# Moving the node projection behind the last transposition of a sort, in program order

## The chip, the core and the metric

The kernel runs on one core of one Trainium2 chip. The metric is the device time of one execution in microseconds (us), as the median of several runs. A ratio in this document is the mean time of one kernel's fast runs over the mean of the other's fast runs of the same rounds, so it is not quite the ratio of the quoted medians.

The engines are called by their names in the profile: PE is TensorE (PEld its weight loads), DVE is VectorE, ACT is ScalarE, SP is SyncE, whose queue (SPq) issues DMAs here.

## The reference

A message-passing layer over a graph with 4096 nodes and 262,144 edges:

```python
N, E, D = 4096, 262144, 256
self_out = nodes @ w_self
msg = nodes[edges_src] @ w_msg
agg = np.zeros((N, D), dtype=np.float32)
np.add.at(agg, edges_dst, msg)
return self_out + agg
```

## The kernel before

The kernel has three stages. First it loads the edges, packs each edge into one number (key) and brings the 2048 columns of keys into an order with a sorting network. VectorE does the compare steps (minimum and maximum). Now and then the data has to be moved between partitions; TensorE does that by a matmul with a rotated identity matrix, and ScalarE copies the result back. Second, the *projection*: `Y = nodes @ w_msg`, in 32 blocks of 128 rows. It needs the transposed nodes `XT`, which 64 transposing DMAs bring. Third, the counting stage builds one-hot matrices from the sorted keys on VectorE, counts pairs with matmuls, and multiplies the counts with `Y`. The counting stage needs both the end of the sort and `Y`.

The parts that matter here (cuts marked):

```python
# the transposed nodes: 64 DMAs on SyncE's queue                       (line 195)
for t in range(T):                                    # T = 32
    for k in range(2):
        nc.sync.dma_start(
            XT[:, k, t * P:(t + 1) * P],
            nodes_bf_dram[t * P:(t + 1) * P, k * P:(k + 1) * P],
            transpose=True,
        )

psum_y = tc.alloc_tile_pool(name="psum_y", bufs=1, space=bass.MemoryType.PSUM)
for t in range(T):                                    # the projection
    y_ps = psum_y.tile([P, D], FP32, name="y_ps", tag="y_ps", bufs=2)
    for k in range(2):
        nc.tensor.matmul(                             # line 205
            out=y_ps[:], lhsT=XT[:, k, t * P:(t + 1) * P], rhs=wcat[:, 2 + k, :],
            start=(k == 0), stop=(k == 1),
        )
    nc.scalar.copy(out=Y[:, t, :], in_=y_ps[:])       # line 209

psum_sort = tc.alloc_tile_pool(name="psum_sort", bufs=1, space=bass.MemoryType.PSUM)
own = _run_sort(nc, psum_sort, XA, XS, id2, plan, halo)
# ... keys -> run numbers, transpositions, then the counting stage
```

```python
def _run_sort(nc, psum, XA, XS, id2, plan, halo):
    # ...
    for op in SORT_A:
        x, y = XA[a], XA[1 - a]
        if op[0] == "b":
            gap(x, y, op[1])                          # compare steps on VectorE
        # ... "q4": the same idea as below with another view (lines 610, 614)
        elif op[0] == "q16":
            # ...
            for t in range(4):
                tp = psum.tile([P, 512], FP32, name="tp_sw", tag="tp", bufs=4)
                for g in range(4):
                    # ...
                    nc.tensor.matmul(...)             # line 622: a "sort matmul"
                nc.scalar.copy(...)                   # line 626
        # ...
    for t in range(0, nk, 4):                         # the sort's last transposition
        # ...
            nc.tensor.transpose(...)                  # line 645
        nc.scalar.copy(...)                           # line 648
    a = 0
    for h, b, (s0, n0), (s1, n1) in plan:             # VectorE alone, the sort's tail
        # ...
```

The kernel is written against a framework that traces these calls, finds the dependencies and then *emits* one stream of instructions for each engine. The source text is only its input.

Of the kernel before, what the change touches and what calls it, by code (L numbers as in the profile page):

```python
# [9 lines left out]
P = 128  # L10
FP32 = mybir.dt.float32
# [40 lines left out]
def kernel(  # L52
# [9 lines left out]
    nc = tc.nc  # L62

    N, D = nodes.shape
# [4 lines left out]
    T = N // P  # L69
# [13 lines left out]
    wcat = feat.tile([P, 4, D], BF16, name="wcat")  # L83
    XT = feat.tile([P, 2, N], BF16, name="XT")
    Y = feat.tile([P, T, D], BF16, name="Y")
# [7 lines left out]
    plan, halo = _tail_plan(SORT_S)  # L93
    TOT = NCOL + 2 * halo
    sortp = tc.alloc_tile_pool(name="sortp", bufs=1)
    XA = [sortp.tile([P, FP + NCOL + BP], FP32, name=f"XA{i}") for i in range(2)]
    XS = [sortp.tile([P, TOT], FP32, name=f"XS{i}") for i in range(2)]
    id2 = sortp.tile([P, 2 * P], FP32, name="id2")
# [100 lines left out]
            )  # L199

    psum_y = tc.alloc_tile_pool(name="psum_y", bufs=1, space=bass.MemoryType.PSUM)
    for t in range(T):
        y_ps = psum_y.tile([P, D], FP32, name="y_ps", tag="y_ps", bufs=2)
        for k in range(2):
            nc.tensor.matmul(  # L205
                out=y_ps[:], lhsT=XT[:, k, t * P:(t + 1) * P], rhs=wcat[:, 2 + k, :],
                start=(k == 0), stop=(k == 1),
            )
        nc.scalar.copy(out=Y[:, t, :], in_=y_ps[:])  # L209

    psum_sort = tc.alloc_tile_pool(name="psum_sort", bufs=1, space=bass.MemoryType.PSUM)
    own = _run_sort(nc, psum_sort, XA, XS, id2, plan, halo)

    k16 = meta.tile([P, G16], FP32, name="k16")
    k16i = meta.tile([P, G16], I32, name="k16i")
# [19 lines left out]
    own = own[:, halo:halo + NCOL]  # L235
# [20 lines left out]
        out=wr[:], in0=sl[:], scalar1=float(RING), scalar2=float(-RING * BW),  # L256
# [5 lines left out]
        out=poff[:], in0=poff[:], scalar1=2, scalar2=PSUM0,  # L262
        op0=ALU.logical_shift_left, op1=ALU.bitwise_or,
    )
    for t in range(G16 // 4):
        tp = psum_sort.tile([P, 512], FP32, name="tp_sw", tag="tp", bufs=4)
        for k in range(4 * t, 4 * t + 4):
            s = slice(k * P, (k + 1) * P)
            nc.vector.tensor_scalar(
                out=rel[:, s], in0=own[:, s], scalar1=g7f[:, k:k + 1], scalar2=32640.0,  # L270
# [4 lines left out]
            out=vals[:].rearrange("p (q k) -> p q k", k=G16)[:, :, 4 * t:4 * t + 4],  # L275
            in_=tp[:].rearrange("p (k q) -> p q k", k=4),
# [125 lines left out]
    with tc.manual_schedule():  # L402
# [52 lines left out]
        out=bad[0:1, 0:1], in0=gi[0:1, 0:1], scalar=float(W - 1), in1=bad[0:1, 0:1],  # L455
# [7 lines left out]
        out=btot[:], in0=bsum[:, 1:2], scalar=float(E), in1=bsum[:, 0:1],  # L463
# [68 lines left out]
def _tail_plan(gaps):  # L532

    a, e = 0, 2048
    plan = []
    for h in reversed(gaps):
        b = h & -h
        passes = []
        for par in (1, 0):
            i0 = (a - h) // b  # L540
            i0 += (i0 - par) % 2
            i1 = -(-e // b) - 1
            i1 -= (i1 - par) % 2
            passes.append((i0 * b, (i1 - i0) // 2 + 1))
            a = min(a, i0 * b)
            e = max(e, i1 * b + b + h)
        plan.append((h, b, passes[1], passes[0]))
    halo = -(-max(-a, e - 2048) // 128) * 128
    return plan[::-1], halo


def _blocks(x, start, n, b):
    v = x[:, start:start + 1]
    return bass.AP(tensor=v.tensor, offset=v.offset, ap=[list(v.ap[0]), [2 * b, n], [1, b]])


def _run_sort(nc, psum, XA, XS, id2, plan, halo):
    n_col = 2048
    mm = nc.vector.tensor_tensor

    def pair(lo, up, lo_out, up_out):
        mm(out=lo_out, in0=lo, in1=up, op=ALU.min)  # L562
        mm(out=up_out, in0=lo, in1=up, op=ALU.max)  # L563

    def gap(x, y, m):
        b = m & -m
        if m <= PADM:
            n = n_col // (2 * b)
            for par, u in ((0, x), (1, y)):
                s = FP + par * b  # L570
                up = _blocks(u, s + m, n, b)
                pair(_blocks(x, s, n, b), up, _blocks(y, s, n, b), up)
            return
        n = (n_col - m) // b
        k = (n_col - 2 * m) // b
        for par in (0, 1):
            cnt, cin = (n + 1 - par) // 2, (k + 1 - par) // 2
            s, f = FP + par * b, FP + (par + 2 * cin) * b
            lows = [(s, cin), (f, cnt - cin)]
            if par == 0:  # L580
                mm(
                    out=_blocks(y, s, cnt, b), in0=_blocks(x, s, cnt, b),
                    in1=_blocks(x, s + m, cnt, b), op=ALU.min,
                )
            for i, (st, c) in enumerate(lows):
                if not c:
                    continue
                lo = _blocks(x, st, c, b)
                up = _blocks(y if par == 1 and i == 0 else x, st + m, c, b)
                if par == 1:  # L590
                    mm(out=_blocks(y, st, c, b), in0=lo, in1=up, op=ALU.min)
                mm(
                    out=_blocks(x if par == 0 and i == 0 else y, st + m, c, b),
                    in0=lo, in1=up, op=ALU.max,
# [6 lines that stand above are left out]
            gap(x, y, op[1])  # L601
        elif op[0] == "q4":
            bb, rots = op[1:]
# [3 lines that stand above are left out]
                    r = rots[4 * t + g]  # L607
                    c = FP + 512 * t
                    sel = lambda v: v.rearrange("p (i g b) -> p i g b", g=4, b=bb)[:, :, g, :]
                    nc.tensor.matmul(  # L610
                        out=sel(tp[:]), lhsT=id2[:, (P - r) % P:(P - r) % P + P],
                        rhs=sel(x[:, c:c + 512]), start=True, stop=True,
                    )
                nc.scalar.copy(out=y[:, c:c + 512], in_=tp[:])  # L614
        elif op[0] == "q16":
            bb, rots = op[1:]
            sel = lambda v: v[:, FP:FP + n_col].rearrange("p (i g b) -> p g i b", g=16, b=bb)
# [3 lines that stand above are left out]
                    r = rots[4 * t + g]  # L621
                    nc.tensor.matmul(  # L622
                        out=tp[:, g * P:(g + 1) * P], lhsT=id2[:, (P - r) % P:(P - r) % P + P],
                        rhs=sel(x)[:, 4 * t + g], start=True, stop=True,
                    )
                nc.scalar.copy(  # L626
                    out=sel(y)[:, 4 * t:4 * t + 4],
                    in_=tp[:].rearrange("p (g i b) -> p g i b", g=4, b=bb),
                )
        elif op[0] == "sh":  # L630
            bb, mask = op[1:]
            v = x[:, FP:FP + n_col].rearrange("p (i g b) -> p i g b", g=2, b=bb)[:, :, 1, :]
            nc.vector.stream_shuffle(out=v, in_=v, mask=mask)
            continue
        else:
            nc.vector.transpose(out=y[:, FP:FP + n_col], in_=x[:, FP:FP + n_col])
        a = 1 - a
    x = XA[a]
    nk = (n_col + 2 * halo) // P
    for t in range(0, nk, 4):  # L640
        w = min(4, nk - t)
        tp = psum.tile([P, 512], FP32, name="tp_sw", tag="tp", bufs=4)
        for k in range(t, t + w):
            c = FP + k - halo // P
            nc.tensor.transpose(
                tp[:, (k - t) * P:(k - t + 1) * P], x[:, c:c + 16 * (P - 1) + 1:16], id2[:, 0:P]
            )
        nc.scalar.copy(out=XS[0][:, t * P:(t + w) * P], in_=tp[:, 0:w * P])
    a = 0
    for h, b, (s0, n0), (s1, n1) in plan:  # L650
        x, y = XS[a], XS[1 - a]
        for s, n, u in ((halo + s0, n0, x), (halo + s1, n1, y)):
            up = _blocks(u, s + h, n, b)
            pair(_blocks(x, s, n, b), up, _blocks(y, s, n, b), up)
        a = 1 - a
    return XS[a]
# [30 lines left out]
```

## Time and profile before

| | before |
|---|---|
| time, median of 3 (range) | 609.61 us (609.27 to 610.24) |
| span of the profiled run | 606.5 us |
| first compare steps on VectorE end | 69.15 us |
| first sort matmul starts | 117.78 us |
| VectorE goes on with the sort | 124.15 us |
| sort's tail on VectorE | 233.4 to 283 us |
| first one-hot of the counting stage | 292.03 us |

From the page of the kernel before: the span cut into 40 equal slices, each digit the busy share of the slice in tenths.

```profile
span 606.5 us, 10333 instructions
...
PE   0013332410434123001799999999999999999997
...
DVE  3999500079564865999999999898989889898940
```

The right half is the counting stage, with both engines nearly full. On the left VectorE has a hole of three empty slices, from about 76 to 121 us, while TensorE is 20 to 40% busy. The list of waits says what ended it. Each line gives the waiting engine and line, what it waited for, us in total, how often, and the longest single wait.

```profile
PE y_ps L205 <- DMA XT<-nodes_bf_dram: 92.8, 64, 37.2
...
DVE XA L562 <- ACT XA L626: 62.0, 2, 55.0
```

VectorE waited 55.0 us once for ScalarE's copy of a sort matmul. But the copy only came late because the matmul came late. TensorE's timeline around it (start, duration, engine, line, operation; in brackets the idle time before it and what ended that):

```profile
117.59 0.40 PE L205 MATMUL y_ps<-wcat,XT 128*128 128x256 bf16 x1 [0.86 <-DMA XT<-nodes_bf_dram]
117.78 1.53 PE L622 MATMUL tp_sw<-XA,id 128*128 128x128 f32 x6
```

VectorE's timeline:

```profile
68.95 0.20 DVE L592 TENSOR_TENSOR XA<-XA 128x44 f32<-128x44 f32 x1
124.15 1.23 DVE L562 TENSOR_TENSOR XA<-XA 128x1024 f32<-128x1024 f32 x1 [55.00 <-ACT XA L626]
```

The data of the first sort matmul was there at 69.15 us. It started 0.19 us behind the start of the last of the 64 projection matmuls, and it has no idle time of its own: it stood behind them in TensorE's stream. The projection matmuls are not slow, they wait. The views of the lines concerned (durations in ns: least, median, greatest; then the first and the last start in us):

```profile
L205 PE MATMUL y_ps<-wcat,XT x64: 392/393/397, 37.2 to 117.6; 128*128 128x256 bf16 x64
```

```profile
L195 SPq DMA_TRANSPOSE XT<-nodes_bf_dram x64: 1207/1232/1242, 34.8 to 115.2; - x64
```

Each of the 64 transpositions holds its queue for 1.23 us, they start 1.28 us apart ((115.2 − 34.8) / 63), and their data lands 2.3 us after the issue (median). So the last projection matmul can't run before 117.6 us, and whatever stands behind it in TensorE's stream can't either. The Trainium skill ("TensorE: Matmul & The Clock Gate", Part 2) says that matmuls stay in program order, which we read as the order of the engine's own instruction stream. The trace agrees: the first sort matmul, ready at 69.15 us, starts at 117.78 us.

One more thing is to be read from VectorE's timeline: the order in which instructions run is not that of the source. These are two stretches of it.

```profile
26.35 0.77 DVE L581 TENSOR_TENSOR XA<-XA 128x595 f32<-128x595 f32 x1
27.04 0.16 DVE L181 TENSOR_SCALAR ta<-ta 128x16 int32<-128x16 int32 x1
...
27.63 0.17 DVE L185 CUSTOM_DVE_ANT_0 lo_c<-ta,tb 128x32 uint16<-128x32 uint16 x1
...
291.44 0.17 DVE L458 TENSOR_REDUCE bcol<-bad 128x1 f32<-128x16 f32 x1
...
292.03 0.69 DVE L305 TENSOR_TENSOR e_oh<-slo_b,jrow 128x1024 bf16<-128x1024 int16 x1
```

Line 581 belongs to the sort, which the source calls after lines 181 and 185, yet it runs before them. Line 458 stands in the source behind the whole counting stage, yet it runs ahead of that stage's first one-hot (line 305). The framework fills each engine's stream with what is ready.

### The profile page before, as it was taken

Reading aid. Unit: us, or ns where it says so; the run is one execution under the profiler, and the core shown is the slowest. Engines: PE = TensorE matmul, PEld = TensorE weight load, DVE = VectorE, ACT = ScalarE, POOL = GpSimd, SP = SyncE. Lnnn points to the kernel's source line nnn. Section 1 sums busy time; section 2 is a strip of 40 time slices with the busy share of each in tenths; the row PEclk is TensorE's granted clock in tenths of the full one; section 3 lists DMA queues with packets and bytes.
Section 4 is the critical chain, followed back from the end, with each engine's and each line's share of the span. In section 5 each row is a group of like instructions: output and inputs, shape, how many; then the busy total and the mean of one; then the engine's idle time right before and its main releaser. Section 6 shows DMA issues by size and latency. Waiting matters only on the chain.

```text
span 606.5 us, 10333 instructions
## 1 busy us (share of the span) xinstructions
PE 365.0 (60%) x4113; PEld 324.4 (53%) x4113; DVE 461.1 (76%) x388; ACT 274.4 (45%) x792; POOL 9.7 (2%) x28
## 2 busy tenths in 40 slices
PE   0013332410434123001799999999999999999997
PEld 0000000310334123000698989898988989898986
DVE  3999500079564865999999999898989889898940
ACT  2001111110111012000387878777878777787886
POOL 6000000000000000000000000000000000000000
PEclk9999999975657577555699999999999999999999
DMA  9921111000000000000000000000000000000000
GB/s 312 197 80 26 25 25 26 21 0 0 0 0 0 1 1 1 0 0 1 0 2 29 1 28 2 28 2 28 2 28 3 26 28 2 28 1 29 1 28 22
DMA packets 24356, 15.66 MB, mean 26 GB/s; under 512 B 10994, under 2 KB 23794, under 8 KB 23794
## 3 DMA queue, kind: packets, MB, share of 16 engines
q1 hardware_dynamic: 19362, 10.51, 5.8%
q0 software_dynamic: 4656, 2.36, 2.9%
q10 hardware_dynamic: 288, 2.10, 0.9%
q8 instruction: 34, 0.56, 0.4%
q14 instruction: 16, 0.13, 0.1%
HBM read 8.92 MB, written 6.30 MB: 25 GB/s over the span
## 4 chain that ended last, share of the span: by engine, by line
PE 51%; DVE 22%; SPq 13%; DMA 5%; ACT 5%; issue 2%; POOL 1%; ACTq 0%; DVEq 0%; POOLq 0%
PE ring L333 21%; PE out_ps L390 17%; SPq L195 13%; DVE XA L562 6%; DVE XA L563 6%; PE out_ps L385 6%; DVE XS L563 4%; DVE XS L562 4%; ACT at L359 3%; PE tp_sw L610 3%; DMA nodes_bf<-in_nodes_dram 3%; PE tp_sw L622 2%; DMA nodes_bf_dram<-nodes_bf 2%; PE out_ps L378 1%; ACT o_sb L399 1%
## 5 line engine op out<-in xcount | busy, mean ns | idle before, releaser
L359 ACT ACTIVATE at<-ring 128x496 bf16<-128x496 f32 (+1 forms) x352 | 202.0, 574 | 69.7 <-PE ring L333 68.2
L390 PE MATMUL out_ps<-Y,at 128*128 128x256 bf16 x1024 | 169.0, 273 | 0.0
L305 DVE TENSOR_TENSOR e_oh<-slo_b,jrow 128x4096 bf16<-128x4096 int16 (+2 forms) x68 | 147.1, 2164 | 28.8 <-PE ring L333 27.4
L333 PE MATMUL ring<-d_oh,e_oh 128*128 128x112 bf16 x2048 | 164.0, 214 | 2.7 <-DVE d_oh L305 2.7
L333 PEld LDWEIGHTS <-e_oh 128*128 128x128 bf16 x2048 | 138.4, 98 | 6.6 <-issue 2.5
L305 DVE TENSOR_TENSOR d_oh<-rel_b,jrow 128x3584 bf16<-128x3584 int16 (+2 forms) x68 | 129.7, 1907 | 0.0
L390 PEld LDWEIGHTS <-at 128*128 128x128 bf16 x1024 | 99.3, 97 | 8.3
L385 PE MATMUL out_ps<-Y,at 128*128 128x256 bf16 (+1 forms) x351 | 95.2, 271 | 0.0
L333 PE MATMUL ring<-zer 128*128 128x224 bf16 x352 | 91.8, 261 | 0.7 <-ACT vals L274 0.7
L562 DVE TENSOR_TENSOR XA<-XA 128x1024 f32<-128x1024 f32 x15 | 18.4, 1226 | 82.4 <-ACT XA L626 62.0
L205 PE MATMUL y_ps<-wcat,XT 128*128 128x256 bf16 x64 | 25.2, 394 | 92.8 <-DMA XT<-nodes_bf_dram 92.8
L359 ACT ACTIVATION_READ_ACCUMULATOR at<-ring 128x1 f32 x352 | 68.7, 195 | 0.0
L205 PEld LDWEIGHTS <-XT 128*128 128x128 bf16 x64 | 6.7, 104 | 111.0 <-DMA XT<-nodes_bf_dram 111.0
L209 ACT CAST Y<-y_ps 128x256 bf16<-128x256 f32 x32 | 11.9, 372 | 91.3 <-PE y_ps L205 91.3
L610 PE MATMUL tp_sw<-XA,id 128*128 128x128 f32 x96 | 17.6, 365 | 37.7 <-DVE XA L563 37.7
L610 PEld LDWEIGHTS tp_sw<-XA,id 128*128 128x128 f32 x96 | 17.1, 278 | 38.2 <-issue 38.2
L333 PEld LDWEIGHTS <-zer 128*128 128x128 bf16 x352 | 34.7, 98 | 5.0 <-issue 0.9
L273 PE MATMUL tp_sw<-ident,XS 128*128 128x128 f32 x16 | 4.7, 452 | 53.8 <-DVE qb L164 53.8
L385 PEld LDWEIGHTS <-at 128*128 128x128 bf16 (+1 forms) x351 | 34.8, 99 | 1.0 <-issue 0.8
L273 PEld LDWEIGHTS tp_sw<-ident,XS 128*128 128x128 f32 x16 | 2.9, 183 | 55.4 <-issue 54.4
L622 PE MATMUL tp_sw<-XA,id 128*128 128x128 f32 x64 | 11.9, 367 | 31.0 <-DVE XA L563 31.0
L614 ACT COPY XA<-tp_sw 128x512 f32<-128x512 f32 x12 | 7.0, 585 | 48.3 <-PE tp_sw L610 48.3
(99 smaller groups left out, 257.0 us busy)
## 6 DMA issues: line engine op xcount, KB each, us to landing
out_dram<-o_sb SPq DMA_DIRECT2D x11, 256.0 KB, 2.2
s<-in_edges_src_dram ACTq DMA_DIRECT2D x2, 1024.0 KB, 10.2
d<-in_edges_dst_dram SPq DMA_DIRECT2D x2, 1024.0 KB, 10.4
nodes_bf<-in_nodes_dram POOLq DMA_DIRECT2D x1, 2048.0 KB, 17.6
nodes_bf_dram<-nodes_bf SPq DMA_DIRECT2D x1, 2048.0 KB, 9.5
out_dram<-o_sb SPq DMA_DIRECT2D x10, 128.0 KB, 2.1
XT<-nodes_bf_dram SPq DMA_TRANSPOSE x64, 2.3
wcat<-in_w_self_dram POOLq DMA_DIRECT2D x1, 128.0 KB, 12.1
```

Of the source, the lines that this page charges most:

```text
L195: nc.sync.dma_start(XT[:, k, t * P:(t + 1) * P], nodes_bf_dram[t * P:(t + 1) * P, k * P:(k + 1) * P], transpose=True,)
L205: nc.tensor.matmul(out=y_ps[:], lhsT=XT[:, k, t * P:(t + 1) * P], rhs=wcat[:, 2 + k, :], start=(k == 0), stop=(k == 1),)
L209: nc.scalar.copy(out=Y[:, t, :], in_=y_ps[:])
L305: tt(out=o[:, 0:n // 2], in0=val[:, c:c + n].rearrange("p (g i) -> p g i", i=2).unsqueeze(2).to_broadcast(shp), in1=jrow[:, 0:wid, :].unsq ...
L333: mm = nc.tensor.matmul(out=ap, lhsT=lhsT, rhs=rhs, start=start, stop=True, skip_group_check=True,).ins
L359: ins = nc.scalar.activation(out=at[:, 0:n], in_=ring[:, b:b + n], func=ACTF.Copy, accum_out=csum[:, r:r + 1],).ins
L385: nc.tensor.matmul(out=out_ps[0:m, 0, :], lhsT=at_of.pop(r - 1)[:, w:w + m], rhs=Y[:, b, :], start=False, stop=False, skip_group_check=True,)
L390: nc.tensor.matmul(out=out_ps[:, t, :], lhsT=at[:, t * P:(t + 1) * P], rhs=Y[:, b, :], start=False, stop=(b == NB - 1), skip_group_check=True,
L562: mm(out=lo_out, in0=lo, in1=up, op=ALU.min)
L563: mm(out=up_out, in0=lo, in1=up, op=ALU.max)
L610: nc.tensor.matmul(out=sel(tp[:]), lhsT=id2[:, (P - r) % P:(P - r) % P + P], rhs=sel(x[:, c:c + 512]), start=True, stop=True,)
L622: nc.tensor.matmul(out=tp[:, g * P:(g + 1) * P], lhsT=id2[:, (P - r) % P:(P - r) % P + P], rhs=sel(x)[:, 4 * t + g], start=True, stop=True,)
```

## The change

The intent was to close the hole: let the sort matmuls stand ahead of the projection in TensorE's stream. The projection would run under the sort's tail, where TensorE and ScalarE have nothing to do for 50 us. The code of the projection is put into a function, and the sort calls it behind its last transposition.

```diff
-    for t in range(T):
-        y_ps = psum_y.tile([P, D], FP32, name="y_ps", tag="y_ps", bufs=2)
-        ...
-        nc.scalar.copy(out=Y[:, t, :], in_=y_ps[:])
+
+    def project():
+        for t in range(T):
+            y_ps = psum_y.tile([P, D], FP32, name="y_ps", tag="y_ps", bufs=2)
+            ...
+            nc.scalar.copy(out=Y[:, t, :], in_=y_ps[:])
 
     psum_sort = tc.alloc_tile_pool(name="psum_sort", bufs=1, space=bass.MemoryType.PSUM)
-    own = _run_sort(nc, psum_sort, XA, XS, id2, plan, halo)
+    own = _run_sort(nc, psum_sort, XA, XS, id2, plan, halo, project)
@@ _run_sort, behind the loop of the last transposition
         nc.scalar.copy(out=XS[0][:, t * P:(t + w) * P], in_=tp[:, 0:w * P])
+    project()
     a = 0
     for h, b, (s0, n0), (s1, n1) in plan:
```

No operation is added or removed, and no dependency.

More of the change, by code (lines that the diff above doesn't have):

```diff
@@ L201 @@
     psum_y = tc.alloc_tile_pool(name="psum_y", bufs=1, space=bass.MemoryType.PSUM)
-    for t in range(T):
-        y_ps = psum_y.tile([P, D], FP32, name="y_ps", tag="y_ps", bufs=2)
-        for k in range(2):
-            nc.tensor.matmul(
-                out=y_ps[:], lhsT=XT[:, k, t * P:(t + 1) * P], rhs=wcat[:, 2 + k, :],
-                start=(k == 0), stop=(k == 1),
-            )
-        nc.scalar.copy(out=Y[:, t, :], in_=y_ps[:])
+    def project():
+        for t in range(T):
+            y_ps = psum_y.tile([P, D], FP32, name="y_ps", tag="y_ps", bufs=2)
+            for k in range(2):
+                nc.tensor.matmul(
+                    out=y_ps[:], lhsT=XT[:, k, t * P:(t + 1) * P], rhs=wcat[:, 2 + k, :],
+                    start=(k == 0), stop=(k == 1),
+                )
+            nc.scalar.copy(out=Y[:, t, :], in_=y_ps[:])
     psum_sort = tc.alloc_tile_pool(name="psum_sort", bufs=1, space=bass.MemoryType.PSUM)
-    own = _run_sort(nc, psum_sort, XA, XS, id2, plan, halo)
+    own = _run_sort(nc, psum_sort, XA, XS, id2, plan, halo, project)
     k16 = meta.tile([P, G16], FP32, name="k16")
@@ L554, in _blocks, with _run_sort @@
     return bass.AP(tensor=v.tensor, offset=v.offset, ap=[list(v.ap[0]), [2 * b, n], [1, b]])
-def _run_sort(nc, psum, XA, XS, id2, plan, halo):
+def _run_sort(nc, psum, XA, XS, id2, plan, halo, project):
     n_col = 2048
```

## The prediction

> **What bounds the kernel now.** The span is 606.5 us. From about 300 us TensorE is above 90% busy (the 40-slice view); that counting stage is not touched. Before it stands the sort. The list of waits shows its one big hole: VectorE (L562) waits 55.0 us for the ScalarE copy L626. The timeline shows why: VectorE's first run of compare stages ends at 69.15 us, but the first sort matmul (L622) starts at 117.78 us, 0.19 us behind the start of the last projection matmul (L205, 117.59 us). All 64 projection matmuls stand ahead of it in TensorE's stream, and each waits for its DMA transposition (92.8 us in 64 waits; one transposition each 1.27 us, 34.8 to 117.5 us). The Trainium skill ("TensorE: Matmul & The Clock Gate", Part 2) says matmuls stay in program order; the trace agrees. The chain of waits accordingly runs over the transposition queue (13%).
>
> **What the change would be worth if the emitted order followed the program.** The first sort matmuls would start at about 69.3 us instead of 117.8: 48.5 us saved, all on the chain. The projection would lie under VectorE's last sort stage (233.4 to 283 us, 50 us, TensorE and ScalarE idle): 64 matmuls at 0.2 to 0.4 us and 32 copies of 0.37 us, an estimate of 15 to 25 us, hidden. Total about 561 us, an 8% gain.
>
> **Why I do not expect it.** The builder does not emit instructions in program order: it fills each engine's stream with what is ready in its own model of time, and the program order only decides between ready instructions. The trace of before shows it on VectorE: the sort's L581 starts at 26.35 us ahead of L181 and L185 (27.04 and 27.63 us), which the program states earlier; and L449 to L458, which the program states behind the whole counting stage, run at 290.4 to 291.4 us, ahead of its first one-hot (L305, 292.03 us). So a late place in the program does not keep an instruction late. Early on TensorE's only ready work is the projection, and all of it was emitted ahead of L622. With an order by readiness the builder must have believed the transpositions done before the sort's first matmul is ready; that belief does not change with the move. The projection depends on nothing of the sort, so moving its text adds no dependency. I expect the same stream on TensorE and ScalarE: L205 (new line number) ahead of the first sort matmul, the same 55 us wait, nothing removed, added or moved.
>
> **Predicted time: 609.6 us, 8 in 10 between 607 and 612.** Chances: faster by over 2% 0.10, within 2% 0.89, slower by over 2% 0.01.
>
> **What would show it right.** VectorE's wait for the first sort copy stays at about 55 us; the projection matmuls still start from 37.2 to 117.6 us; the first sort matmul still starts at about 117.8 us; the counting stage starts at about 292 us.
>
> **What would show it wrong.** The first sort matmul at about 69 us, the 55 us wait shrunk to about 6.5 us, as the later ones of its kind (6.2 to 7.4 us), the projection matmuls between about 184 and 235 us, and a time near 561 us. That happens if the builder keeps TensorE's order by program for these instructions, or if a PSUM slot or its model's timing holds the projection back until sort matmuls are ready. A partial hoist would give something between.

## The result, and the profile after

| | before | after |
|---|---|---|
| time, median (range), 4 runs each | 609.44 us (609.16 to 610.24) | 607.79 us (606.9 to 609.52) |
| span of the profiled run | 606.5 us | 606.1 us |
| projection matmuls start | 37.2 to 117.6 us | 37.1 to 117.5 us |
| first sort matmul starts | 117.78 us | 117.65 us |
| VectorE's wait before the sort goes on | 55.00 us | 54.79 us |
| first one-hot | 292.03 us | 291.58 us |

The ratio is 0.9974, with a 95% interval of 0.995 to 0.9998: the same within 2%, but with an interval that leaves out 1. The experiments come back to that.

The lines of the kernel after that answer to those of before; its line numbers are 2 higher in these parts. The page:

```profile
span 606.1 us, 10333 instructions
...
PE   0013332410434123001799999999999999999997
...
DVE  3999500089564866999999999898989889898940
```

The waits, with the hole unchanged at 54.8 us:

```profile
PE y_ps L207 <- DMA XT<-nodes_bf_dram: 92.6, 64, 37.1
...
DVE XA L564 <- ACT XA L628: 61.7, 2, 54.8
```

TensorE's and VectorE's timelines at the same place:

```profile
117.46 0.40 PE L207 MATMUL y_ps<-wcat,XT 128*128 128x256 bf16 x1 [0.85 <-DMA XT<-nodes_bf_dram]
117.65 1.75 PE L624 MATMUL tp_sw<-XA,id 128*128 128x128 f32 x7
```

```profile
68.87 0.20 DVE L594 TENSOR_TENSOR XA<-XA 128x44 f32<-128x44 f32 x1
123.86 1.23 DVE L564 TENSOR_TENSOR XA<-XA 128x1024 f32<-128x1024 f32 x1 [54.79 <-ACT XA L628]
```

The projection still stands ahead of the sort matmuls. The two emitted programs were then compared instruction by instruction, on every engine: opcode, operands, PSUM banks (PSUM is the memory that the matmuls write to), waits and signals are equal in all of them. Only source line numbers and generated names differ. The change altered the source and not the program.

### The profile page after: what moved, and what is told of

Read it like the earlier page. It is cut to its first block, busy times and chain, and to the rows that moved or that the text cites. A ratio compares the mean times of both kernels' runs of the same rounds, so it can differ in the third digit from the quotient of the medians.

```text
span 606.1 us, 10333 instructions
## 1 busy us (share of the span) xinstructions
PE 364.7 (60%) x4113; PEld 324.1 (53%) x4113; DVE 461.3 (76%) x388; ACT 274.4 (45%) x792; POOL 9.7 (2%) x28
## 4 chain that ended last, share of the span: by engine, by line
PE 51%; DVE 22%; SPq 13%; DMA 5%; ACT 5%; issue 2%; POOL 1%; ACTq 0%; DVEq 0%; POOLq 0%
PE ring L335 21%; PE out_ps L392 17%; SPq L195 13%; DVE XA L565 6%; DVE XA L564 6%; PE out_ps L387 6%; DVE XS L565 4%; DVE XS L564 4%; ACT at L361 3%; PE tp_sw L612 3%; DMA nodes_bf<-in_nodes_dram 3%; PE tp_sw L624 2%; DMA nodes_bf_dram<-nodes_bf 2%; PE out_ps L380 1%; ACT o_sb L401 1%
## 5 line engine op out<-in xcount | busy, mean ns | idle before, releaser
L275 PEld LDWEIGHTS tp_sw<-ident,XS 128*128 128x128 f32 x16 | 2.9, 182 | 55.5 <-issue 54.4
```

## The experiments

What the framework emits on TensorE up to the counting stage, read from each built kernel, in matmuls and transpositions in order ("sort 1" and "sort 2" are the two groups of 16 of line 622, "sort 3 to 5" the 48 of line 610, "last" the 32 of line 645, "keys" the 16 behind the tail; the profile shows two records for each of these sort matmuls, so a group of 16 appears there as x32):

```
before, after, prio, keep_before:  64 projection, sort 1, sort 2, sort 3 to 5, last, keys
pin, keep_after:                   sort 1, sort 2, sort 3 to 5, last, 64 projection, keys
ahead24:                           48 projection, sort 1, sort 2, sort 3 to 5, last, 16 projection, keys
held:                              sort 1 with 28 projection strewn in behind its 4th, 36 projection,
                                   sort 2, sort 3 to 5, last, keys
```

Two questions were open. First, is the hole on VectorE really nothing but TensorE's issue order, and what is it worth? Second, why did the move of the text not change that order? Theory A: the framework emits what is ready in its own model of time, and program order decides only between ready instructions. The rivals were that something else makes the hole, or that program order or priority decides the order after all. All eight runs gave correct results. The first four kernels ran on one chip, beside 11 runs of the kernel before (608.42 us median, 607.17 to 609.83); the other four on another chip, beside 7 runs of it (607.99 us, 607.24 to 609.59).

### pin: the order edge that the move lacked

```diff
-            nc.tensor.transpose(
+            last = nc.tensor.transpose(
                 tp[:, (k - t) * P:(k - t + 1) * P], x[:, c:c + 16 * (P - 1) + 1:16], id2[:, 0:P]
             )
 ...
-    project()
+    with tc.issue_after(last.ins):     # order of issue on TensorE, no wait
+        project()
```

(`tc` is passed into `_run_sort` for it.)

> The changed kernel plus an order edge (issue order only, no wait): every projection matmul is queued behind the last transposition of the sort on TensorE. Theory A (the 55 us hole is only TensorE's issue order): first sort matmul at about 69.3 us, VectorE's wait before it about 6.5 us, projection between 184 and about 205 us under VectorE's tail, counting stage from about 243 us, time about 561 us (ratio 0.92). Rival B (the hole has another cause, such as a transfer that the sort matmuls or their copies wait for, or the projection can't be hidden in the tail): time between 585 and 610 us.

Measured: 560.13 us median (559.61 to 561.2, 5 runs), ratio 0.9211 (0.9194 to 0.9229). VectorE's timeline at the place of the hole:

```profile
68.94 0.20 DVE L594 TENSOR_TENSOR XA<-XA 128x44 f32<-128x44 f32 x1
75.57 1.23 DVE L564 TENSOR_TENSOR XA<-XA 128x1024 f32<-128x1024 f32 x1 [6.43 <-ACT XA L628]
```

And the view of the line of the projection matmuls in the same kernel:

```profile
L207 PE MATMUL y_ps<-wcat,XT x64: 269/270/273, 183.7 to 197.1; 128*128 128x256 bf16 x64
```

The wait fell from 55.00 to 6.43 us. That is 48.57 us, and the median fell by 48.29 us (608.42 − 560.13). The gain arrives whole, because everything up to the counting stage is one chain: the first one-hot moved from 292.03 to 243.25 us.

```profile
243.25 0.69 DVE L307 TENSOR_TENSOR e_oh<-slo_b,jrow 128x1024 bf16<-128x1024 int16 x1
```

The projection now takes 14.0 us (from its first matmul at 183.71 us to the end of its last copy at 197.75 us, early in a tail that begins at 184.65 us and lasts 50 us) and holds nobody up. Its matmuls take 270 ns instead of 393 each; why was not tested. They now run closely one behind the other on data that is long there, but the sort matmuls, too, take 415 ns early in an unbroken run and 273 ns late in it (last section), so a change of clock is a likely cause. This is the version that beats both kernels. Rival B is out: nothing but the order made the hole.

### after_again and before_again: how far identical programs stray

No edit: the kernel after once more, and the kernel before timed against itself.

> The changed kernel once more. Its emitted instructions equal those of before in opcode, operands, PSUM banks, waits and signals on every engine, source line numbers and instruction names apart. Theory A (same program): ratio 1.000 within 0.3%, and the 0.26% of the first comparison is scatter. Rival B (something in it is really faster): ratio 0.997 again, with an interval that excludes 1.

> The kernel before against itself: shows how far a ratio of identical programs strays from 1. Expected 1.000 within 0.3%.

Measured: after_again 608.17 us (607.52 to 610.01, 6 runs), ratio 1.0001 (0.9982 to 1.0021); before_again 608.17 us (607.75 to 610.06, 6 runs), ratio 1.0007 (0.9987 to 1.0027). The 0.26% of the first comparison did not come back, and no difference between the programs exists that could have made it. It was scatter, though its interval left out 1. The interval came from four runs a side; with differences this small it should not be trusted alone.

### ahead24: part of the projection ahead, part behind

As pin, with the first 24 of 32 row blocks stated ahead of the sort, where the framework keeps them ahead:

```diff
-    def project():
-        for t in range(T):
+    def project(t0=24, t1=T):
+        for t in range(t0, t1):
 ...
+    project(0, 24)
     psum_sort = tc.alloc_tile_pool(name="psum_sort", ...)
```

> As the pinned kernel, but the projection of the first 24 of 32 row blocks stands ahead of the sort's matmuls and only the last 8 are pinned behind them. Theory A (the last transposition that stands ahead decides): the 48th projection matmul started at 97.2 us in before, so the first sort matmul starts at about 97.5 us, VectorE's first wait is about 35 us, and the time is 609.5 minus 20.3, about 589 us. Rival B (any projection ahead costs the whole hole, or none does): 609 or 561 us.

Measured: 587.69 us (586.7 to 589.84, 5 runs), ratio 0.9669 (0.9647 to 0.9692). TensorE's timeline and, below it, VectorE's waits:

```profile
97.52 0.40 PE L207 MATMUL y_ps<-wcat,XT 128*128 128x256 bf16 x1 [0.84 <-DMA XT<-nodes_bf_dram]
97.71 5.04 PE L625 MATMUL tp_sw<-XA,id 128*128 128x128 f32 x32
```

```profile
DVE XA L565 <- ACT XA L629: 40.5, 2, 33.9
```

The first sort matmul starts 0.19 us behind the start of the last projection matmul that stands ahead of it, here the 48th, as in the kernel before behind the 64th. VectorE's wait is 33.9 us, 21.1 less than before. The sort starts when the data of the last projection matmul ahead has come. The time fell by 20.7 us; expected were 20.3.

### keep_after and keep_before: program order kept on purpose

The framework can be told to keep program order for chosen engines. In keep_after this is put around the sort (and with it the moved projection); in keep_before around both the projection at its old place and the sort:

```diff
+    with tc.manual_schedule(engines={mybir.EngineType.PE, mybir.EngineType.Activation}):
-    own = _run_sort(nc, psum_sort, XA, XS, id2, plan, halo, project)
+        own = _run_sort(nc, psum_sort, XA, XS, id2, plan, halo, project)
```

```diff
+    with tc.manual_schedule(engines={mybir.EngineType.PE, mybir.EngineType.Activation}):
-    for t in range(T):
-        y_ps = ...
+        for t in range(T):
+            y_ps = ...
 ...
-    own = _run_sort(nc, psum_sort, XA, XS, id2, plan, halo)
+        own = _run_sort(nc, psum_sort, XA, XS, id2, plan, halo)
```

> The changed kernel with TensorE and ScalarE told to keep program order over the sort and the projection. Theory A (the move failed only because the builder reorders): the projection is emitted behind the sort's last transposition, and the time is as with the pinned kernel, about 561 us. Rival B: the change itself is worthless and this stays at 609 us.

> The kernel before (projection stated ahead of the sort) with TensorE and ScalarE told to keep program order over the projection. Theory A: keeping order is not itself a gain, the place of the text counts once order is kept: 609 us, all 64 projection matmuls from 37 to 118 us, first sort matmul at 117.8 us. Rival B (keeping order helps by itself, by different waits): well under 609 us.

Measured: keep_after 560.97 us (559.35 to 561.84, 4 runs), ratio 0.9216 (0.919 to 0.9242); keep_before 609.48 us (607.32 to 610.28, 4 runs), ratio 1.0009 (0.9982 to 1.0037). The view of the projection's tile in keep_after:

```profile
L207 PE MATMUL y_ps<-wcat,XT x64: 269/270/273, 185.7 to 199.0; 128*128 128x256 bf16 x64
```

And VectorE's waits for the copies of the sort matmuls, first in keep_after, then in keep_before:

```profile
DVE XA L565 <- ACT XA L629: 14.5, 2, 7.3
...
DVE XA L563 <- ACT XA L627: 63.2, 2, 55.8
```

The edit under study is in keep_after unaltered. With program order kept it gives the whole gain; without it, none. Keeping order gives nothing by itself. keep_before is the program of before, and keep_after that of pin, in every instruction (names of registers apart). So the two kernels of about 560 us are one program, timed on two chips.

### prio: a higher priority for the sort

```diff
-    own = _run_sort(nc, psum_sort, XA, XS, id2, plan, halo)
+    with tc.high_priority():
+        own = _run_sort(nc, psum_sort, XA, XS, id2, plan, halo)
```

> The kernel before with the sort traced at raised priority. Theory A (the builder takes what is ready in its model, priority decides only between ready instructions): the emitted stream still has all 64 projection matmuls ahead of the first sort matmul, 609 us, VectorE's wait about 55 us. Rival B (a low priority of the sort is what puts the projection first): 561 us.

Measured: 608.1 us (607.09 to 609.17, 4 runs), ratio 0.9994 (0.9968 to 1.002). VectorE's waits in it:

```profile
DVE XA L563 <- ACT XA L627: 62.8, 2, 55.5
```

The hole is still 55.5 us, and TensorE's stream is emitted as before in every instruction. The priority did act elsewhere: on VectorE line 181, which started at 27.04 us before, now stands behind more of the sort.

```profile
26.57 0.77 DVE L582 TENSOR_TENSOR XA<-XA 128x595 f32<-128x595 f32 x1
...
30.88 0.17 DVE L181 TENSOR_SCALAR ta<-ta 128x16 int32<-128x16 int32 x1
```

This fits theory A: priority reorders what is ready together, and was of no help where the favoured instruction is not yet ready when the choice falls.

### held: make the transpositions late in the framework's model too

The transpositions and the projection are both traced right ahead of the first sort matmul, and each transposition is made to wait for the last compare step on VectorE before it (a real wait):

```diff
+    def load_and_project(after):
+        for t in range(T):
+            for k in range(2):
+                tr = nc.sync.dma_start(XT[...], nodes_bf_dram[...], transpose=True)
+                tc.add_manual_dep(tr.ins, after.name, mybir.DependencyInfo(
+                    mybir.DependencyClass.Sync, mybir.DependencyReason.DATA), reason="hold")
+        ...                                  # then the projection, as before
 @@ _run_sort
         elif op[0] == "q16":
+            if load_and_project:             # first time only
+                load_and_project(last[0])    # last[0]: the last compare step traced
+                load_and_project = None
```

> The transpositions are made to wait for the last VectorE instruction ahead of the first sort matmul; the projection is still stated ahead of that sort matmul in the program. Theory A (readiness in the builder's model, which takes the transpositions to be far quicker than they are): the emitted stream has 4 sort matmuls first, then 28 projection matmuls strewn between the other 12 of that group, then 36 before the second group. On the chip the transpositions run from about 69.5 to 152 us, the first group ends at about 107 us (28th transposition), VectorE waits about 39 us there and about 21 us for the second group (64th transposition, about 152.5 us), and the time is about 607 us, near the same total as before from two holes in place of one. Rival B (program order decides): all 64 projections ahead of the first sort matmul, which starts at about 152 us, time about 644 us.

Measured: 606.4 us (606.03 to 607.88, 4 runs), ratio 0.9975 (0.995 to 1.0). VectorE's timeline and the view of the projection's tile:

```profile
107.72 2.49 DVE L564 TENSOR_TENSOR XA<-XA 128x1024 f32<-128x1024 f32 x2 [38.30 <-ACT XA L634]
...
158.06 2.48 DVE L564 TENSOR_TENSOR XA<-XA 128x1024 f32<-128x1024 f32 x2 [20.12 <-ACT XA L634]
```

```profile
L207 PE MATMUL y_ps<-wcat,XT x64: 392/393/396, 71.8 to 152.2; 128*128 128x256 bf16 x64
```

This is the mirror image of the change. There, instructions stated late were emitted early; here sort matmuls stated after the projection are emitted before it, because in the framework's model they are ready first. So program order binds in neither direction. The strewing also suggests that the model is off: it puts 28 projection matmuls among 12 sort matmuls of about 0.4 us each, as if transpositions came at least that quickly, while on the chip they come 1.28 us apart ((152.2 − 71.8) / 63). The one hole of 55.0 us and the ordinary wait of 7.0 us for the second group (62.0 us on that line of the waits before) became two holes of 38.3 and 20.1 us (58.4 us), and the time stays within 2 us of before. The waits (about 39 and 21 us) and the time (about 607 us) were expected so. The order expected is right to the matmul, but an order can be read from a build without the chip, and the record doesn't say whether it was.

## Why the prediction was right

- **Where the hole comes from.** Right, and shown. The prediction read it from two neighbouring lines of TensorE's timeline; pin took the projection away from that place alone, and the wait fell to 6.43 us (stated: about 6.5).
- **What the order would be worth if it followed the program.** The prediction said 48.5 us and about 561 us. The program with that order, as pin and as keep_after, ran at 560.13 and 560.97 us. The projection's own length was put too high: an estimate of 15 to 25 us, measured 14.0 us. It is hidden in a tail of 50 us, so the error cost nothing.
- **That the order would not follow the program.** Right, and shown. The emitted program is equal to before in every operand, wait and signal. The reason given, that readiness in the framework's model decides, is supported by three kernels together: the change (stated late, emitted early), held (stated early, emitted late) and prio (raised priority, same order). Program order and priority are out as the sole rule; an order that only goes along with readiness, such as one by the length of the chain of dependencies, was not tested. That the model takes the transpositions for quicker than they are was inferred from the order before, and the strewing in held fits it. How the model times a transposition was not measured.
- **The time.** 609.6 us were predicted (the median of the kernel before), between 607 and 612; 607.79 us were measured, and 608.17 us in the repeat. The small drop is no effect of the change: the programs are the same, and the repeat's ratio is 1.0001.

What was decisive was to doubt the diff. The gain computed from the trace, 8%, was correct to within 1 us, and the edit as written was still worth nothing.

## What to carry to other kernels

When a framework schedules for you, moving a call in the source changes an engine's stream only if the framework keeps that order: look in the trace for instructions that already run out of source order, and compare the emitted streams before you time anything. A filler (work that could run at any time, here the projection) whose data comes late on the chip but early in the scheduler's model can be put in front of critical work. Here an explicit order edge, or kept program order for those engines, fixed it, and a higher priority did not. And the cost of standing behind such a filler was here the arrival of its last input: 64 projection matmuls ahead made a wait of 55.0 us, 48 made one of 33.9 us, although the 64 are busy for only 25.2 us.

## What the Trainium skill lacked or had wrong

- The pages on TensorE and on reading traces do not say that the order of an engine's stream can be a scheduling framework's choice and not the source's, or that an order edge may be needed. "TensorE: Matmul & The Clock Gate" (Part 2) says that matmuls stay in program order, which is true of the emitted stream alone: the same source order ran at 608.17 us as emitted by readiness and at 560.97 us with program order kept.
- "DMA: Bandwidth & Descriptors" (Latency and other measured facts) gives 261 GB/s for transposing DMAs, measured in one kernel with a non-contiguous middle dimension, and does not say how far apart many small ones come on this chip. Here 64 transpositions of 128x128 bf16 (32 KB each) on one queue came 1.28 us apart, which is 25.7 GB/s, a tenth of that.
- "TensorE: Matmul & The Clock Gate" (Part 1) says that an idle array is throttled, and that its clock events in a trace can be unreliable. The pinned kernel agrees on both. Its second group of sort matmuls, after 31.0 us of idle time on TensorE, took 415 ns (median) from 105.9 to about 110 us, where the profile shows a granted clock of 0.50, and 273 ns from 111 us on, where it shows 1.00. Its first group, after 69 us without any work on TensorE, also took 415 ns up to about 72.8 us and 273 ns after that, but the profile shows 1.00 all the way from 0 to 79 us. So here a 1.00 ahead of the first dense work did not mean full speed; the page does not name this case.
